# The residual of the output projection: an accumulating DMA in place of a load and a VectorE addition

## The chip, the core and the metric

The kernel runs on one core of a Trainium2 chip. The metric is the device time of one launch, in microseconds (us). TensorE (PE in the profile) multiplies matrices, VectorE (DVE) and ScalarE (ACT) work element by element, GpSimd (POOL) and SyncE (SP) do little arithmetic here or none: SP issues DMAs, the transfers between device memory (DRAM) and the core's on-chip memory. Each engine works through its own list of instructions in order, and waits at an instruction until what it needs is there.

## The reference

A two-layer encoder for 512 tokens of width 2048. In each layer `h` is the RMS-normalised `x`, one projection feeds three groups of attention heads (16 heads in all), the heads' outputs are multiplied by gates, and one output projection is added to `x`. A final RMS norm follows.

```python
for l in range(DEPTH):                       # DEPTH = 2
    h = rms_norm(x, norm_g[l])
    z = h @ w_in[l]
    ...                                      # three kinds of attention: o_na, o_dl, o_m
    y = jnp.concatenate([o_na * jax.nn.silu(na_g), o_dl * jax.nn.silu(dl_g), o_m * jax.nn.silu(m_g)], axis=-1)
    x = x + y @ w_out[l]
return rms_norm(x, final_g)
```

The change concerns the last line of the loop: how `x +` is done.

## The kernel before

**Layout.** Activations lie transposed: 16 tiles (`KO`) of 128 model columns by 512 tokens, f32. Every product is made of three products of split operands: `split` (L179, L180) writes `hi`, the operand rounded by a ScalarE cast, and `lo`, the rest, by a VectorE subtraction; `mm3` (L204 to L206) multiplies hi·hi, hi·lo, lo·hi.

**Weights.** A weight tile is 128 output columns by all 2048 rows, streamed in two halves of 128 x 1024. `next_half` keeps `AHEAD` = 3 halves loaded (SP, L153) and split (ACT L179, DVE L180) ahead of the one in use; the raw halves `wr` and both parts `wh`, `wl` have four buffers each (`W_BUFS`). So the cast of a half can begin when the half four places before it has been used up, and its result is wanted three halves later. In the program a half's load and split come ahead of the products that use the half three places before it.

**The stage of the change.** At the end of a layer a loop over `j` makes the new `x` tile by tile (L511 to L529): 16 tiles in layer 0, 13 in layer 1 (the last three of layer 1 are made in two halves of the tokens by `project`, which the change leaves alone). For tile `j`, SP loads the old `x` (L520; from the input `xT` in layer 0, from the scratch `xs` in device memory in layer 1) into a tile `p`; TensorE computes the projection `acc` in 48 products (`gemm_t`, L521); VectorE adds both into `x` (L523). What follows from `x`:

- `add_square` (L524): ScalarE squares the tile (L242 or L245), VectorE adds the square into `ssq` (L247), the sum that the next RMS norm needs.
- in layer 0, SP stores `x` to `xs` (L526), and `act_tile` (L527) multiplies it by the norm's gain and splits it for the next layer (ACT L185, DVE L186);
- in layer 1, ScalarE multiplies it by the final gain (L529).

**Behind the stage.** Layer 1's first product (`gemm_v`) starts right after layer 0's last tile. It takes the new tiles in order, two for each half of a weight tile, and at its second half `rms_scales` comes in: TensorE sums `ssq` down the partitions (L267), VectorE makes the reciprocal root (L252 to L258, L274), TensorE spreads it (L275), ScalarE copies it to `rstd` (L277).

**What sets the order.** The code is one stream of instructions; a scheduler spreads it over the engines' lists, moving a few instructions by its own estimate of times, and inserts the waits. GpSimd has nothing to do in the loop; its list holds attention masks before it and the two products of the rotary tables (L480, L481) behind it.

Of the kernel before, what the change touches and what calls it, by code (L numbers as in the profile page):

```python
# [14 lines left out]
ALU = mybir.AluOpType  # L15
# [5 lines left out]
T = 512  # L21
D = 2048
# [5 lines left out]
EPS = 1e-6  # L28
NEG = -1e30
ROWS = 8  # L30
W_HALF = 1024  # columns of half a weight tile
W_BUFS = 4  # halves of weight tiles on chip, as loaded and in each of their two parts
AHEAD = 3  # halves that are loaded and split ahead of the one in use
U_BUFS = 62  # [128, 512] tiles for everything that lives longer than a few instructions
LAST = 3  # column tiles of the last projection that are computed for one half of the tokens after the other
WARM = 10  # products of constants ahead of the first loads' arrival
# Microseconds of TensorE's work from a head's operands to its first scores, between its steps, and from
# its last scores to its first transposes.
NA_TIMES = (5.0, 1.2, 3.0)
DIL_TIMES = (8.0, 1.3, 4.0)  # L40
MEM_TIMES = (4.0, 0.7, 3.5)
# Tiles of x that are loaded along with each of the first halves of the weights.
FIRST_LOADS = (1, 3, 2, 2, 2, 2, 2, 2)

# Column tiles of one layer's weights, in the order in which they are streamed: "T" tiles hold 128
# output columns and all of K, "V" tiles 512 output columns and a quarter of K.
SEQ = (
# [14 lines left out]
for _key in SEQ:  # L62
    WPOS[_key] = sum(4 if s in ("v", "mv") else 1 for s, _ in SEQ[:len(WPOS)])
# Mix tiles (heads) in the order in which gates are applied: memory, neighbourhood, dilated.
MIX = [("m", h) for h in range(H_M)] + [("na", h) for h in range(H_NA)] + [("dl", h) for h in range(H_DL)]
# Neighbourhoods of a query block of 16 grid columns: the key tiles that they touch, the first of the 32
# columns that they span, where these columns' biases start in a head's window, and their mask.
NA_KB = [(0, 2), (0, 3), (1, 4), (2, 4)]
# [7 lines left out]
def hybrid_kernel(ctx: ExitStack, tc: tile.TileContext, xT, memT, gains, rpbw, wts, cs_tab, dil_tab, na_tab, outT):  # L76
# [35 lines left out]

# [1 line left out]
    ones = cpool.tile([P, P], F32, tag="ones", name="ones")  # L114
# [15 lines left out]
    ssq = cpool.tile([P, T], F32, tag="ssq", name="ssq")  # L130
    # TensorE's clock is raised by work: raise it while the first loads are under way.
    bank = sc_bank()
# [3 lines left out]

# [1 line left out]
    stream = []  # L138
# [38 lines left out]
    def split(x, hi, lo):  # L177
        """x as hi + lo."""
        nc.scalar.copy(hi, x)  # L179
        nc.vector.tensor_tensor(lo, x, hi.bitcast(F32), ALU.subtract)  # L180
        return hi, lo

    def split_scaled(x, g, hi, lo):
        """x * g (one g per partition) as hi + lo."""
        nc.scalar.activation(hi, x, AF.Copy, scale=g)  # L185
        nc.vector.scalar_tensor_tensor(lo, x, g, hi.bitcast(F32), ALU.mult, ALU.subtract)  # L186
        return hi, lo

    # Attention is issued in steps between the matmuls of later products. A step is due when TensorE has
    # had work for so many microseconds since the head's operands were issued that its inputs are there.  # L190
    clock = [0.0]
# [10 lines left out]
    def mm3(out, a, b, start, stop):  # L202
        """out += a.T @ b for a = a[0] + a[1], b = b[0] + b[1]."""
        nc.tensor.matmul(out, lhsT=a[0], rhs=b[0], start=start, stop=False)  # L204
        nc.tensor.matmul(out, lhsT=a[0], rhs=b[1], start=False, stop=False)  # L205
        nc.tensor.matmul(out, lhsT=a[1], rhs=b[0], start=False, stop=stop)  # L206
        clock[0] += 3 * out.shape[-1] / 2400.0

    def gemm_t(l, key, act, n=T):
        """[128 columns, n tokens] of one T tile."""  # L210
        acc = acc_bank()
        for half in range(2):
            hi, lo = next_half(l, key)
            for k8 in range(8):
                ko = half * 8 + k8
                sl = slice(k8 * P, (k8 + 1) * P)
                mm3(acc[:, :n], (hi[:, sl], lo[:, sl]), act[ko], ko == 0, ko == KO - 1)
                pump()
        return acc

    def gemm_v(l, key, act, ntok, hook=None):
        """[ntok x 128 tokens, 512 columns] of one V chunk."""
        accs = [acc_bank() for _ in range(ntok)]
        for q in range(8):
            hi, lo = next_half(l, key)
            if hook is not None:
                hook(q)
            for t in range(ntok):
                ts = slice(t * P, (t + 1) * P)
                for kk in range(2):  # L230
                    ko = 2 * q + kk
                    sl = slice(kk * 512, (kk + 1) * 512)
                    mm3(accs[t], (act[ko][0][:, ts], act[ko][1][:, ts]), (hi[:, sl], lo[:, sl]),
                        ko == 0, ko == KO - 1)
                    pump()
        return accs

# [1 line left out]
    def add_square(src, first, n=T, acc=None):  # L239
# [9 lines left out]
    def rsqrt(out, src_ps, n):  # L249
        """out = (src / D + EPS) ** -0.5"""  # L250
        a = sb.tile([P, 4], F32, tag="rs", bufs=4, name=nm("rs"))[:, :n]
        nc.vector.tensor_scalar(a, src_ps, 1.0 / D, EPS, ALU.mult, ALU.add)  # L252
        u = sb.tile([P, 4], F32, tag="rs", bufs=4, name=nm("rs"))[:, :n]
        nc.vector.tensor_scalar(out.bitcast(I32), a.bitcast(I32), -0.5, 1597463007.0, ALU.mult, ALU.add)
        for _ in range(3):
            nc.vector.tensor_tensor(u, out, out, ALU.mult)
            nc.vector.scalar_tensor_tensor(u, u, -0.5, a, ALU.mult, ALU.mult)
            nc.vector.scalar_tensor_tensor(out, u, 1.5, out, ALU.add, ALU.mult)  # L258

    def rms_scales(bc, tok, n, *accs):  # L260
        """1 / rms of each token: down the partitions in tok, along every partition's row in bc.
        The sum of accs holds the squares, to be summed down the partitions."""
        nt = n // P
# [15 lines left out]

# [1 line left out]
    def attend(q, score, v, order, first, gap, wait):  # L281
        """Queue a head's steps and return its tile of outputs [hd, queries].
        score(qt): probabilities of a query tile; order: key tile, [(query tile, its column there)]."""
        out, probs, pts, bank = [], {}, {}, []
# [37 lines left out]
    def softmax(s, neg_max, scale, src):  # L322
        """s = exp(scale * src + neg_max) over its row's sum."""
        l = stat()
        nc.scalar.activation(s, src, AF.Exp, bias=neg_max, scale=scale, accum_out=l)  # L325
        r = stat()
        nc.vector.reciprocal(r, l)
        nc.vector.tensor_scalar(s, s, r, None, ALU.mult)
# [53 lines left out]

# [1 line left out]
    def act_tile(l, ko, x):  # L384
# [10 lines left out]
    for l in range(NL):  # L395
# [15 lines left out]
        def beside_first(q):  # L411
            """What runs beside a layer's first product: norms, the memory's split, layer 0's loads and splits."""
            if l == 0:
                tiles = range(len(act), min(2 * q + 4, KO))
                for ko in tiles:
                    act.append(act_tile(0, ko, xraw[ko]))
                for ko in tiles:
                    add_square(xraw[ko], ko == 0)
            if q == (6 if l == 0 else 1):
                rms_scales(rstd, rstd_tok, T, ssq)  # L420
# [71 lines left out]

        # gates
        mix = []
# [13 lines left out]

        # output projection, residual, and what follows from a tile of the new x
        act = []  # L510
        out = []  # L511
        kept = []
        for j in range(KO if l + 1 < NL else KO - LAST):
            if l + 1 == NL and j == KO - LAST - 4:
                for c in range(4):
                    raw = u32()
                    nc.sync.dma_start(out=raw, in_=wts[l, WPOS["o", KO - LAST], :, c * T:(c + 1) * T])
                    kept.append(split(raw, u32r(), u32r()))
            old = f32t("p", 4)
            nc.sync.dma_start(out=old, in_=xT[j] if l == 0 else xs[j])  # L520
            acc = gemm_t(l, ("o", j), mix)  # L521
            x = u32()
            nc.vector.tensor_tensor(x, acc, old, ALU.add)  # L523
            add_square(x, j == 0)  # L524
# [6 lines left out]

# [1 line left out]
    cols = range(KO - LAST, KO)  # L533
# [53 lines left out]
def _tables(np):  # L587
    """Constants of the shapes alone: rotary tables and attention masks."""
    tok = np.arange(T).reshape(ROWS, GRID_W).T.reshape(T)
# [88 lines left out]
```

## Time and profile before

| | |
|---|---|
| time, median of 2 runs | 1868.47 us (1868.43 and 1868.52) |
| span of the profiled execution, first to last instruction | 1868.0 us |
| TensorE busy | 1849.4 us (99%) |
| VectorE, ScalarE, GpSimd busy | 1038.4, 659.4, 51.6 us |
| granted TensorE clock, mean | 0.996 of full speed |
| tiles that the change touches | 16 in layer 0, 13 in layer 1 |

The profile is of one execution. Its own time is not listed apart from its span; the runs' median lies 0.47 us above that span, which is what lies around it. A row of a timeline gives the start in us from the first instruction, the duration in us, the engine, the line of the code, the operation, output<-input with the names of the code, and in brackets the idle time ahead of it with what ended it. A group of rows in the tables is one kind of instruction. Matmuls are pipelined, so one matmul of the stage shows 0.39 us although one starts about every 0.23 us.

### The profile page before, as it was taken

What the parts mean: (1) busy time and instruction counts of PE and PEld (TensorE: products, weight loads), DVE (VectorE), ACT (ScalarE), POOL (GpSimd) and SP (SyncE); (2) the same over time, 40 slices, a digit from 0 to 9 for tenths busy, and PEclk for the clock granted to TensorE, in tenths of its full rate; (3) what the DMA queues carried; (4) which work ended last, traced back from release to release, by engine and by line L of the source; (5) the groups of instructions that cost most, each with busy time, mean ns of one, the idle gap of its engine ahead of it and who ended that gap; (6) DMA issues with size and microseconds to landing.
All of it is one profiled execution on the core that took longest, in us unless ns stands there. A gap on an engine that the chain in (4) does not pass through costs nothing.

```text
span 1868.0 us, 22192 instructions
## 1 busy us (share of the span) xinstructions
PE 1849.4 (99%) x8828; PEld 1548.2 (83%) x8828; DVE 1038.4 (56%) x1577; ACT 659.4 (35%) x1034; POOL 51.6 (3%) x110
## 2 busy tenths in 40 slices
PE   9999999999999999999999999999999999999997
PEld 7888888888888888888888898888888888888887
DVE  7457552564567787543434565435636677883333
ACT  6346442333233323232323453333323333233331
POOL 0113000100000000000000100000000000000000
PEclk9999999999999999999999999999999999999998
DMA  8334423222223333444423353232232233334422
GB/s 288 93 101 150 140 68 101 88 80 80 90 68 103 101 94 98 133 138 146 126 92 93 120 172 101 79 102 70 78 91 79 68 103 101 92 100 124 124 91 91
DMA packets 67175, 198.67 MB, mean 106 GB/s; under 512 B 7040, under 2 KB 16768, under 8 KB 67072
## 3 DMA queue, kind: packets, MB, share of 16 engines
q1 hardware_dynamic: 67072, 197.26, 34.4%
q8 instruction: 69, 1.13, 0.2%
q14 instruction: 34, 0.28, 0.0%
HBM read 188.84 MB, written 8.39 MB: 106 GB/s over the span
## 4 chain that ended last, share of the span: by engine, by line
PE 95%; DVE 2%; DMA 1%; ACT 1%; issue 1%; SPq 0%; DVEq 0%; ACTq 0%
PE acc L204 28%; PE acc L205 28%; PE acc L206 28%; PE sc L294 2%; PE pv L205 1%; PE pv L204 1%; PE pv L206 1%; PE sc L205 1%; PE sc L206 1%; PE sc L204 1%; DVE u L186 1%; DMA wr<-in_wts 1%; DMA u<-in_memT 0%; DVE wl L180 0%; ACT u L185 0%
## 5 line engine op out<-in xcount | busy, mean ns | idle before, releaser
L204 PE MATMUL acc<-u,wh 128*128 128x512 f32 (+1 forms) x2064 | 786.5, 381 | 0.0
L205 PE MATMUL acc<-u,wh 128*128 128x512 f32 (+1 forms) x2064 | 784.3, 380 | 0.0
L206 PE MATMUL acc<-u,wl 128*128 128x512 f32 (+1 forms) x2064 | 783.6, 380 | 0.0
L179 ACT CAST wh<-wr 128x1024 fp32r<-128x1024 f32 (+1 forms) x319 | 334.8, 1049 | 724.5 <-PE acc L205 401.0
L180 DVE TENSOR_TENSOR wl<-wr,wh 128x1024 fp32r<-128x1024 f32 (+1 forms) x319 | 390.1, 1223 | 319.0 <-ACT wh L179 313.6
L206 PEld LDWEIGHTS acc<-u,wl 128*128 128x128 f32 x2064 | 388.2, 188 | 74.4
L205 PEld LDWEIGHTS acc<-u,wh 128*128 128x128 f32 x2064 | 388.5, 188 | 69.1
L204 PEld LDWEIGHTS acc<-u,wh 128*128 128x128 f32 x2064 | 388.5, 188 | 69.0
L204 PE MATMUL acc<-wh,u 128*128 128x512 f32 x448 | 175.3, 392 | 1.3 <-ACT u L185 1.3
L205 PE MATMUL acc<-wl,u 128*128 128x512 f32 x448 | 174.9, 390 | 0.0
L206 PE MATMUL acc<-wh,u 128*128 128x512 f32 x448 | 174.4, 390 | 0.0
L180 DVE TENSOR_TENSOR ptl<-sc,pth 128x512 fp32r<-128x512 f32 (+2 forms) x112 | 67.4, 603 | 89.7 <-ACT pth L179 89.2
L501 DVE RECIPROCAL tmp<-tmp 128x512 f32<-128x512 f32 x32 | 107.2, 3351 | 1.0
L179 ACT CAST pth<-sc 128x512 fp32r<-128x512 f32 (+2 forms) x112 | 57.9, 517 | 122.6 <-PE sc L294 119.9
L204 PEld LDWEIGHTS acc<-wh,u 128*128 128x128 f32 x448 | 84.2, 188 | 17.9 <-ACT u L185 1.5
L206 PEld LDWEIGHTS acc<-wh,u 128*128 128x128 f32 x448 | 84.1, 188 | 18.0
L205 PEld LDWEIGHTS acc<-wl,u 128*128 128x128 f32 x448 | 84.1, 188 | 16.9 <-DVE wl L180 0.4
L325 ACT ACTIVATE p<-p,stat 128x256 f32<-128x256 f32 (+1 forms) x96 | 59.1, 616 | 87.2 <-DVE stat L335 86.4
L523 DVE TENSOR_TENSOR u<-acc,p 128x512 f32<-128x512 f32 x29 | 20.0, 691 | 89.3 <-PE acc L206 89.3
L179 ACT CAST u<-tmp 128x512 fp32r<-128x512 f32 (+1 forms) x64 | 37.7, 591 | 67.2 <-DVE tmp L438 67.2
L294 PEld LDWEIGHTS sc<-ident,p 128*128 128x128 f32 x376 | 48.0, 140 | 15.0
L294 PE MATMUL sc<-ident,p 128*128 128x128 f32 x376 | 59.8, 272 | 0.0
(98 smaller groups left out, 1237.1 us busy)
## 6 DMA issues: line engine op xcount, KB each, us to landing
wr<-in_wts SPq DMA_DIRECT2D x317, 512.0 KB, 3.7
p<-in_xT SPq DMA_DIRECT2D x32, 256.0 KB, 3.5
u<-in_memT SPq DMA_DIRECT2D x16, 256.0 KB, 4.4
xs<-u SPq DMA_DIRECT2D x16, 256.0 KB, 2.0
p<-xs SPq DMA_DIRECT2D x13, 256.0 KB, 2.7
outT<-wr SPq DMA_DIRECT2D x6, 512.0 KB, 3.6
e<-in_rpbw SPq DMA_DIRECT2D x12, 192.0 KB, 2.4
u<-in_wts SPq DMA_DIRECT2D x4, 256.0 KB, 4.2
```

What stands on the lines that cost most here:

```text
L179: nc.scalar.copy(hi, x)
L180: nc.vector.tensor_tensor(lo, x, hi.bitcast(F32), ALU.subtract)
L186: nc.vector.scalar_tensor_tensor(lo, x, g, hi.bitcast(F32), ALU.mult, ALU.subtract)
L204: nc.tensor.matmul(out, lhsT=a[0], rhs=b[0], start=start, stop=False)
L205: nc.tensor.matmul(out, lhsT=a[0], rhs=b[1], start=False, stop=False)
L206: nc.tensor.matmul(out, lhsT=a[1], rhs=b[0], start=False, stop=stop)
L294: nc.tensor.transpose(tr[:, i * P:(i + 1) * P], probs[qt][:, col:col + P], ident)
L325: nc.scalar.activation(s, src, AF.Exp, bias=neg_max, scale=scale, accum_out=l)
L501: nc.vector.reciprocal(e, e)
L523: nc.vector.tensor_tensor(x, acc, old, ALU.add)
```

## The change

The load of the old `x` on SP and the tile `p` for it are gone. ScalarE copies the product from `acc` to `x`, and a DMA issued by GpSimd adds the old `x` from device memory onto `x` where it lies on the chip. The lines behind it are the same and now take `x` when this DMA has ended. In the changed file the lines from here on have numbers one lower (the copy is L521, the DMA L522, the store to `xs` L525). The rest of the diff takes comments out of the file.

```diff
-            old = f32t("p", 4)
-            nc.sync.dma_start(out=old, in_=xT[j] if l == 0 else xs[j])
             acc = gemm_t(l, ("o", j), mix)
             x = u32()
-            nc.vector.tensor_tensor(x, acc, old, ALU.add)
+            nc.scalar.copy(x, acc)
+            nc.gpsimd.dma_start(out=x, in_=xT[j] if l == 0 else xs[j], accum_op=ALU.add)
             add_square(x, j == 0)
             if l + 1 < NL:
                 nc.sync.dma_start(out=xs[j], in_=x)
```

How the lists of the engines move is shown at two places. The first is ScalarE around the last tile of layer 0 (`j` = 15). Before, with `u_7388` the new `x`, `tmp_7390` its square and `u_7394` its part for the next layer; the casts `wh` are weight halves:

```order
L179 CAST wh_7359<-wr_7358 128x1024
L179 CAST wh_7403<-wr_7402 128x1024
L245 ACTIVATE tmp_7390<-u_7388 128x512
L185 ACTIVATE u_7394<-u_7388,g_sb 128x512
L179 CAST wh_7433<-wr_7432 128x1024
L277 COPY rstd<-sc_7456 128x512
```

The same place of the changed kernel, where `u_7371` is the new `x`:

```order
L179 CAST wh_7342<-wr_7341 128x1024
L179 CAST wh_7387<-wr_7386 128x1024
L521 COPY u_7371<-acc_7310 128x512
L245 ACTIVATE tmp_7374<-u_7371 128x512
L185 ACTIVATE u_7378<-u_7371,g_sb 128x512
L179 CAST wh_7417<-wr_7416 128x1024
L277 COPY rstd<-sc_7440 128x512
```

One row is new, the copy; it stands behind the cast that stood ahead of the square, and the square is next to it. Every tile of the loop in layer 0 has this pattern of two casts, copy, square, gain.

The second place is SP's list in layer 0 around three stores of new tiles. Before, `p` is the load of an old tile:

```order
L153 DMA wr_6409<-in_wts 128x1024
L526 DMA xs<-u_6295 128x512
L520 DMA p_6522<-in_xT 128x512
L153 DMA wr_6452<-in_wts 128x1024
L153 DMA wr_6482<-in_wts 128x1024
L526 DMA xs<-u_6366 128x512
L520 DMA p_6595<-in_xT 128x512
```

And of the changed kernel:

```order
L153 DMA wr_6447<-in_wts 128x1024
L525 DMA xs<-u_6293 128x512
L153 DMA wr_6477<-in_wts 128x1024
L153 DMA wr_6519<-in_wts 128x1024
L525 DMA xs<-u_6363 128x512
```

The loads of old tiles are gone from SP's list, and each store stands one weight load later. On GpSimd the 16 accumulating DMAs of layer 0 stand together between the last attention mask of layer 0's list and the rotary products (L480, L481), and the 13 of layer 1 at the list's end. TensorE's list is the same but for the four L275 of layer 1's norm, which stand two products later; VectorE's loses the 29 additions, and a few weight subtractions stand one or two places from where they stood.

## Rows read from the trace of the kernel before

**Rows 1.** The page: span, and busy time, share and instructions of each engine

```profile
span 1868.0 us, 22192 instructions
PE 1849.4 (99%) x8828; PEld 1548.2 (83%) x8828; DVE 1038.4 (56%) x1577; ACT 659.4 (35%) x1034; POOL 51.6 (3%) x110
```

**Rows 2.** The page: the chain that ended last, by engine

```profile
PE 95%; DVE 2%; DMA 1%; ACT 1%; issue 1%; SPq 0%; DVEq 0%; ACTq 0%
```

**Rows 3.** Windows: layer 0's loop, most of layer 1's, the end; columns in the first line

```profile
core 0: us, PE busy (x) PEld busy (x) DVE busy (x) ACT busy (x) POOL busy (x), PEclk, DMA share, GB/s
767.00:930.30 163.30, 163.30 (x722) 135.23 (x721) 65.51 (x74) 48.90 (x61) 0.00 (x0) 1.00 0.45 140
...
1683.00:1804.00 121.00, 121.00 (x535) 100.21 (x534) 43.61 (x48) 39.47 (x48) 0.00 (x0) 1.00 0.43 130
1804.00:1868.00 64.00, 51.29 (x378) 48.78 (x376) 24.18 (x71) 11.23 (x19) 0.00 (x0) 0.89 0.20 66
```

**Rows 4.** Waits of TensorE, first and last of five: for whom, total us, times, longest

```profile
PE sc L275 <- DVE tmp L274: 4.2, 3, 2.6
...
PE sc L267 <- ACT tmp L555: 0.4, 1, 0.4
```

**Rows 5.** Timeline of VectorE from layer 0's tile 14 to the norm

```profile
919.42 0.69 DVE L523 TENSOR_TENSOR u<-acc,p 128x512 f32<-128x512 f32 x1 [3.31 <-PE acc L206]
...
930.30 0.69 DVE L523 TENSOR_TENSOR u<-acc,p 128x512 f32<-128x512 f32 x1 [3.35 <-PE acc L206]
931.16 1.23 DVE L180 TENSOR_TENSOR wl<-wr,wh 128x1024 fp32r<-128x1024 f32 x1 [0.17 <-ACT wh L179]
932.30 0.68 DVE L247 TENSOR_TENSOR ssq<-ssq,tmp 128x512 f32<-128x512 f32 x1
```

**Rows 6.** Timeline of ScalarE over the same stretch

```profile
930.07 1.05 ACT L179 CAST wh<-wr 128x1024 fp32r<-128x1024 f32 x1 [4.38 <-PE acc L205]
931.03 0.62 ACT L245 ACTIVATE tmp<-u 128x512 f32<-128x512 f32 x1
931.56 0.71 ACT L185 ACTIVATE u<-u,g_sb 128x512 fp32r<-128x512 f32 x1
...
941.31 0.59 ACT L277 COPY rstd<-sc 128x512 f32<-128x512 f32 x1 [4.48 <-PE sc L275]
```

**Rows 7.** Timeline of TensorE: layer 1's first product and its norm

```profile
930.10 0.39 PE L204 MATMUL acc<-wh,u 128*128 128x512 f32 x1
...
935.32 0.39 PE L206 MATMUL acc<-wh,u 128*128 128x512 f32 x1
935.54 0.95 PE L267 MATMUL sc<-ones,ssq 128*128 128x1 f32 x8
936.35 0.49 PE L204 MATMUL acc<-wh,u 128*128 128x512 f32 x1
```

**Rows 8.** DMAs by line, first the loads of `p` in layer 0's loop, then the stores

```profile
L520 SPq DMA_DIRECT2D p<-in_xT x12: 328/423/425, 768.5 to 887.9; - x12
...
DMA to landing us min/median/max: 2.6/2.9/4.8
...
L526 SPq DMA_DIRECT2D xs<-u x16: 326/326/331, 767.8 to 931.0; - x16
...
DMA to landing us min/median/max: 2.0/2.0/2.3
```

**Rows 9.** Timeline of GpSimd behind layer 0's loop

```profile
941.98 1.29 POOL L480 TENSOR_TENSOR rope_c<-rope_c,rstd 128x512 f32<-128x512 f32 x1 [570.36 <-ACT rstd L277]
```

**Rows 10.** Timeline of SP at layer 0's last tile

```profile
931.02 0.33 SPq L526 DMA_DIRECT2D xs<-u  x1
932.41 40.84 SPq L153 DMA_DIRECT2D wr<-in_wts  x8
```

**Rows 11.** Line L523 in the whole trace: durations in ns min/median/max

```profile
L523 DVE TENSOR_TENSOR u<-acc,p x29: 683/692/692, 767.1 to 1815.3; 128x512 f32<-128x512 f32 x29
```

## The prediction

> **What bounds the kernel now.** I read the page's totals first. TensorE is busy for 1849.4 us of a span of 1868.0 us [rows 1], so all other engines together hold it up for only 18.6 us. The chain that ended last is 95% TensorE [rows 2], and the list of TensorE's waits holds five short ones, none longer than 2.6 us and none for a weight half or for a tile of the new `x` [rows 4]. Next the windows: in layer 0's loop TensorE is busy for 163.30 of 163.30 us at granted clock 1.00 (2.4 GHz); ScalarE works 48.90 us there, VectorE 65.51 us, GpSimd nothing [rows 3]. Layer 1's loop, of which the second window is most, has no idle TensorE either. So the stage that the change edits is paced by TensorE alone, and an edit off TensorE can win nothing there. It can lose, at a place where TensorE soon needs what comes out of the loop. The timelines show the tightest such place: behind layer 0's last tile. I therefore read the three engines there.
>
> The last two additions start at 919.42 and 930.30 [rows 5]: a tile lasts 10.88 us, a weight half 5.44 us. After tile 15, layer 1's first product starts at once (930.10), and 5.44 us later, at 935.54, TensorE comes to L267, which sums `ssq` [rows 7]. `ssq` is complete at 932.30 + 0.68 = 932.98 [rows 5]. **The slack is 935.54 - 932.98 = 2.56 us.**
>
> **The change, part by part.**
>
> *Removed.* 29 VectorE additions at 0.692 us, 20.1 us [rows 11], and 29 loads on SP with 0.33 to 0.42 us of issue each [rows 8]. VectorE is idle 3.3 us ahead of each addition [rows 5] and SP is not waited for, so this is worth 0.
>
> *Added on ScalarE.* 29 copies from `acc`. The nearest row is L277, also a copy of 128x512 out of TensorE's accumulators: 0.59 us [rows 6], 17.1 us in all. ScalarE does 48.90 / 15 = 3.26 us a tile in the 15 tile periods of layer 0's window [rows 3]; with the copy 3.85 us out of 10.88. That alone costs 0 too.
>
> *Added as a wait.* The square of a tile now waits for copy, GpSimd's issue and the transfer. Call t the time from the copy's end to the square's start. No row of the trace shows t: GpSimd issues no DMA in the loop, and nothing accumulates. The rows near it are the plain load of the same 256 KB, 2.6 to 4.8 us with a median of 2.9, and the store of such a tile, 2.0 us; SP's issue is seen as 0.33 us [rows 8]. An accumulation must read device memory and the tile on the chip, and write the tile. Lower bound: one issue and the quickest of these transfers, 0.33 + 2.0 = 2.3 us. Upper bound: an issue as long as a whole GpSimd operation on such a tile, 1.29 us [rows 9], the slowest load and the slowest store one after the other, 1.29 + 4.8 + 2.3 = 8.4 us. I take the middle reading, both legs at their medians one after the other: **t = 0.33 + 2.9 + 2.0 = 5.2 us**, since the operation does a load's work and moves the tile a second time.
>
> The Trainium skill (DMA: Bandwidth & Descriptors, "Anatomy of one DMA — SWDGE (gpsimd) path") fits a DMA issued from GpSimd as about 2.0 us plus its bytes at 436 GB/s. For 256 KB that makes 2.6 us as an estimate, with which the wait would be just covered and the time 1868.5; no run here shows it, and the fit is of plain copies. The skill's page Collectives: The Full Stack (Part 3) lays the lower rate of a reduction in transfer to its two source reads, which is on the side of the larger t.
>
> *What hides the wait inside the loop.* Behind the waiting square in ScalarE's list stand the gain (L185) and the next two weight casts; VectorE's `ssq` addition and L186 wait too, with weight subtractions behind them. A cast begins when the half four places back is used up (its idle time ends by TensorE, [rows 6]); its result is wanted three halves later, 3 x 5.44 = 16.3 us; cast and subtraction need 1.05 + 1.23 [rows 5, 6]. So 14.0 us of lateness are covered. And a tile's lateness does not pass to the next as long as ScalarE's work and the wait fit into a period: 3.85 + t up to 10.88, so **t up to 7.03 us**. With 5.2, ScalarE is held for 9.05 us of 10.88 and catches up in each tile. Within the loops the price is 0. Where layer 1 prepares its last weight tile, four more casts of 128x512, about 0.62 us each like the square [rows 6], exceed one period by 9.05 + 2.5 - 10.88 = 0.7 us, which the next tile takes up.
>
> *SP.* The store to `xs` waits for the accumulation in place of the addition, and the weight loads behind it wait with it. They now start right behind a split, 932.41 after 931.16 + 1.23 [rows 5, 10], four halves (21.8 us) ahead of their cast; some 5 us of delay are covered. GpSimd has no work in the loop; its next, the rotary products, start at 941.98 after `rstd` [rows 9] and stay where `rstd` is. The accumulation replaces a load of the same bytes, at 0.45 DMA share [rows 3].
>
> *What does not hide it.* At layer 0's end, the cast that begins at 930.07 still stands ahead. The copy takes the square's old place, 931.03, and ends at 931.62; the square starts at 931.62 + t and ends at 932.24 + t. VectorE's addition follows with a handoff of some 0.06 us (I estimate it from 930.99, the end of the addition before, to the square at 931.03 [rows 5, 6]) and takes 0.68, so `ssq` is complete at 932.98 + t. TensorE reaches L267 at 935.54. **Stall = t - 2.56 = 2.7 us**, once. The chain behind L267 (VectorE's root, L275) is shifted whole, and TensorE's products between L267 and L275 cover VectorE's root as before, so nothing more is lost. Layer 1's loop ends differently: its `ssq` is wanted only behind four half tiles of `project`, 4 x 5.44 = 21.8 us after the last tile's end (its addition starts at 1815.3, [rows 11]), so it pays nothing.
>
> The sum: on the profile's span 1868.0 + 2.7 = 1870.7; the runs lie 0.47 us above that span, so 1868.47 + 2.7 = **1871.1 us**.
>
> **The rivals.**
>
> *Hidden altogether.* With t at most 2.56 us, `ssq` is ready when TensorE asks: 1868.5. For it: the lower bound, 2.3, and the 2.0 us of a store. Against it: a load alone takes 2.9 at the median.
>
> *ScalarE becomes the bound (the slower side).* With t over 7.03 us each of 15 periods leaves ScalarE t - 7.03 later, so the last tile's `ssq` comes late by 15 (t - 7.03) + t - 2.56 in all, and TensorE pays that at L267 or, from 14.0 us on, already at a weight half. Layer 1 adds 12 (t - 7.03) + 2.5 - 14.0 where that is positive. At the upper bound, t = 8.4: 20.6 + 5.8 + 4.9 = 31 us, about 1900. It costs 2% (37 us) from t = 8.6 on: 23.6 + 6.0 + 7.3 = 37. For it: the operation is not in the trace, and GpSimd makes the transfer, whose issue I know only from SP; waits of 4.8 us for a plain load occur. Against it: it needs about three median loads' time for 256 KB at a DMA share of 0.45.
>
> *A gain.* The 20.1 us freed on VectorE would count if TensorE waited for VectorE in the loop. It is never idle there [rows 3], and the 12.7 idle us at the end (64.00 - 51.29) lie behind code that the change leaves alone.
>
> **How the numbers follow.** Forecast (t between 2.56 and 7.03; 1868.5 to 1873): 0.72. Hidden: 0.08. ScalarE the bound but under 2% (7.03 to 8.6): 0.08. Over 2%: 0.11. A gain over 2%: 0.01. The prediction is the likeliest, 1871.1. The range takes in the hidden case at 1867.5 and reaches into ScalarE's case up to 1882, which is t = 7.6 (15 x 0.57 + 5.0 = 13.6); beyond it lie some 15 in 100. A change under 2% is about what a measurement of this kernel can't tell from none; so faster 0.01, same 0.88, slower 0.11.
>
> **What would show it.** In the changed profile: TensorE still busy for all of layer 0's loop; one new wait of TensorE, at L267, of t - 2.56; 29 copies of about 0.6 us; ScalarE idle about 5 us ahead of each square, ended by the DMA, and idle again ahead of the first cast behind it. The prediction is wrong if the copies start later and later against the ends of their products, if TensorE waits for weight halves, or if L267 shows no wait.

## The result, and the profile after

The changed kernel takes 1885.73 us (1885.27 and 1886.19), 17.3 us more than before; the ratio is 1.0084, with a 95% interval of 1.0067 to 1.0100. That is under 2%, and outside the range that was forecast (1867.5 to 1882). The span of the profiled execution is 1883.5 us, 15.5 us more than [rows 1].

The page of the changed kernel: span, busy time of the engines, the queue of GpSimd's DMAs (packets, MB, share of 16 engines) and their issues (KB each, median us from issue to landing).

```profile
span 1883.5 us, 22206 instructions
PE 1854.0 (98%) x8828; PEld 1551.7 (82%) x8828; DVE 1018.3 (54%) x1548; ACT 670.0 (36%) x1063; POOL 77.7 (4%) x139
...
q0 software_dynamic: 4176, 7.60, 2.4%
...
u<-in_xT POOLq DMA_DIRECT2D x16, 256.0 KB, 7.3
...
u<-xs POOLq DMA_DIRECT2D x13, 256.0 KB, 7.0
```

VectorE lost 20.1 us of work, as costed. ScalarE's busy time grew by 10.6 us where 17.1 were costed: the 29 copies alone make 16.7, but rows that follow closely overlap, and time in which two overlap counts once. The accumulations need about 7 us to land. TensorE is still busy all through layer 0's loop, as in [rows 3]:

```profile
767.00:930.30 163.30, 163.30 (x722) 135.24 (x721) 52.88 (x56) 51.85 (x72) 13.16 (x15) 1.00 0.50 136
```

The waits of TensorE (total us, times, longest) have two new rows beside those of [rows 4]:

```profile
PE sc L267 <- DVE ssq L247: 6.0, 1, 6.0
PE acc L204 <- ACT u L521: 4.8, 1, 4.8
PE sc L275 <- DVE tmp L274: 4.4, 3, 2.6
```

The first is the wait that was forecast, 6.0 us where 2.7 was written. The second was not: layer 1's first product fills four accumulators at once, and the fourth is the one from which ScalarE still has to copy layer 0's last tile. ScalarE's timeline shows why the copy is late (tiles 1 and 2; L521 is the copy, L245 the square, in brackets the wait ahead of it):

```profile
777.48 1.05 ACT L179 CAST wh<-wr 128x1024 fp32r<-128x1024 f32 x1 [0.87 <-ACT wh L179]
778.43 0.58 ACT L521 COPY u<-acc 128x512 f32<-128x512 f32 x1
786.50 0.63 ACT L245 ACTIVATE tmp<-u 128x512 f32<-128x512 f32 x1 [7.49 <-DMA u<-in_xT]
787.04 0.71 ACT L185 ACTIVATE u<-u,g_sb 128x512 fp32r<-128x512 f32 x1
787.65 1.99 ACT L179 CAST wh<-wr 128x1024 fp32r<-128x1024 f32 x2
789.54 0.57 ACT L521 COPY u<-acc 128x512 f32<-128x512 f32 x1
798.11 0.63 ACT L245 ACTIVATE tmp<-u 128x512 f32<-128x512 f32 x1 [7.99 <-DMA u<-in_xT]
798.65 0.71 ACT L185 ACTIVATE u<-u,g_sb 128x512 fp32r<-128x512 f32 x1
799.26 1.99 ACT L179 CAST wh<-wr 128x1024 fp32r<-128x1024 f32 x2
801.15 0.57 ACT L521 COPY u<-acc 128x512 f32<-128x512 f32 x1
```

From one copy to the next pass 11.11 and 11.61 us, in which ScalarE waits for nothing but the transfer; a tile of TensorE lasts 10.88. Here t, the copy's end to the square's start, is 7.49 and 8.00 us. The list of GpSimd's DMAs gives the sum of the lag (durations of the issue in ns, then first and last start):

```profile
L522 POOL DMA_DIRECT2D u<-in_xT x16: 853/867/1011, 768.5 to 939.1; - x16
```

170.6 us for 15 periods, where 15 x 10.88 = 163.2: the last copy comes 7.4 us late. TensorE's timeline behind it, in the place of [rows 7]:

```profile
933.63 0.39 PE L206 MATMUL acc<-wh,u 128*128 128x512 f32 x1
938.79 0.79 PE L204 MATMUL acc<-wh,u 128*128 128x512 f32 x1 [4.77 <-ACT u L521]
939.38 0.63 PE L205 MATMUL acc<-wl,u 128*128 128x512 f32 x1
...
941.09 0.63 PE L206 MATMUL acc<-wh,u 128*128 128x512 f32 x1
947.69 1.84 PE L267 MATMUL sc<-ones,ssq 128*128 128x1 f32 x8 [5.98 <-DVE ssq L247]
```

The products behind the waits start 0.43 us apart in place of 0.23. The windows show the granted clock (the figure after POOL's):

```profile
930.00:932.00 2.00, 2.00 (x10) 1.68 (x9) 0.00 (x0) 0.00 (x0) 0.00 (x0) 1.00 0.67 165
...
942.00:944.00 2.00, 0.00 (x0) 0.00 (x0) 0.00 (x0) 0.00 (x0) 0.00 (x0) 0.50 0.97 257
...
952.00:954.00 2.00, 2.00 (x6) 1.52 (x6) 1.49 (x8) 0.00 (x0) 0.00 (x0) 0.50 0.67 193
954.00:956.00 2.00, 2.00 (x13) 1.70 (x12) 0.00 (x0) 0.00 (x0) 0.00 (x0) 0.99 0.17 70
```

TensorE stood from about 934 to 938.8, and its clock fell to 0.50 (1.2 GHz) and came back to 0.99 (2.4 GHz) at 954. So the 15.5 us of span are 4.8 + 6.0 of waiting and 4.6 more of busy time (1854.0 against 1849.4), and nearly all of it lies between 934 and 957.

### The profile page after: what moved, and what is told of

Read it like the earlier page. It is cut to its first block, busy times and chain, and to the rows that moved or that the text cites. A ratio compares the mean times of both kernels' runs of the same rounds, so it can differ in the third digit from the quotient of the medians.

```text
span 1883.5 us, 22206 instructions
## 1 busy us (share of the span) xinstructions
PE 1854.0 (98%) x8828; PEld 1551.7 (82%) x8828; DVE 1018.3 (54%) x1548; ACT 670.0 (36%) x1063; POOL 77.7 (4%) x139
## 3 DMA queue, kind: packets, MB, share of 16 engines
q0 software_dynamic: 4176, 7.60, 2.4%
## 4 chain that ended last, share of the span: by engine, by line
PE 86%; issue 6%; DMA 4%; DVE 2%; ACT 2%; POOL 0%; SPq 0%; DVEq 0%; ACTq 0%; POOLq 0%
PE acc L204 25%; PE acc L205 25%; PE acc L206 25%; DMA u<-in_xT 3%; PE sc L294 2%; PE pv L205 1%; PE pv L204 1%; PE pv L206 1%; PE sc L206 1%; PE sc L205 1%; PE sc L204 1%; ACT wh L179 1%; DVE wl L180 1%; ACT u L185 1%; DVE u L186 1%
## 5 line engine op out<-in xcount | busy, mean ns | idle before, releaser
L247 DVE TENSOR_TENSOR ssq<-ssq,tmp 128x512 f32<-128x512 f32 x42 | 28.9, 689 | 186.0 <-ACT tmp L245 186.0
L205 PEld LDWEIGHTS acc<-wl,u 128*128 128x128 f32 x448 | 85.0, 190 | 17.1 <-DVE wl L180 0.5
L245 ACT ACTIVATE tmp<-u 128x512 f32<-128x512 f32 (+1 forms) x42 | 23.1, 550 | 193.6 <-DMA u<-in_xT 116.6
```

What stands on the lines that cost most here:

```text
L245: nc.scalar.activation(sq, src, AF.Square)
L247: eng.tensor_tensor(acc[:, :n], acc[:, :n], sq, ALU.add)
```

## The experiments

Four theories stood at the start. **The wait**: ScalarE, held at each square for a transfer longer than its period allows, falls behind, and TensorE pays for it once, behind layer 0's last tile. Against it: **the copy** (its place on ScalarE costs by itself), **traffic** (the transfers slow the weights, all through both loops), and **the last transfer alone** (no lag, only t ahead of L267). The kernel before, run along, took 1869 to 1872 us from one set of runs to the next, and its spans were 1867.7 to 1870.6. Spans are compared below (1868.0 before, 1883.5 with the change), but one span alone is known to no better than 2 us or so; what rests on less is read from rows.

**The copy alone.** SP's load and VectorE's addition are back, behind ScalarE's copy.

```diff
+            old = f32t("p", 4)
+            nc.sync.dma_start(out=old, in_=xT[j] if l == 0 else xs[j])
             ...
-            nc.gpsimd.dma_start(out=x, in_=xT[j] if l == 0 else xs[j], accum_op=ALU.add)
+            nc.vector.tensor_tensor(x, x, old, ALU.add)
```

> ScalarE copies the product, SP loads the old tile as before, and VectorE adds it in place: the copy without the accumulating DMA. Theory 'ScalarE waits for the transfer in order' (called the wait): nothing but 0.6 us of ScalarE is added per tile and no wait, so 1868.5 within 1 us. Rival 'the copy itself, and its place behind a weight cast, is what costs' (called the copy): about 1885.

Measured: 1869.81 us, span 1868.0, the same as before, and no new wait; the 1.3 us above the expected 1868.5 lie outside the span. The copy is not the cause.

**Each layer alone.** The DMA under `if l == 0` or `if l == 1`, the old lines in the other layer.

> The accumulating DMA in layer 0's 16 tiles only; layer 1 loads and adds as before. The wait: all of the loss inside the span lies behind layer 0's last tile, so the span keeps the +15.5 us, about 1882 to 1884, and the time is about 1884 to 1886. Rival 'it is spread over all 29 tiles': +16/29 of 17.3, about 1878.

> The accumulating DMA in layer 1's 13 tiles only. The wait: ScalarE falls behind there too, but nothing is wanted of it before the lag is made up; span +0 to 1.5 us, and the time about 1869 to 1871.5, the last 1.3 us of it outside the span if the use of GpSimd's DMA queue costs that. Rival 'spread over all 29 tiles': +13/29 of 17.3, about 1876.

Measured: layer 0 alone 1882.79 us, span 1881.0, of the 15.5 us 13.0, a little under what was expected; its waits are 7.7 us at L267 and 3.8 for the accumulator. Part of the missing 2.5 us is a shorter stretch ahead of the first changed line: the first copy starts at 766.0, in the changed kernel at 767.55. Layer 1 alone 1871.69, span 1869.9, with no new wait of TensorE, although ScalarE waits there as in the changed kernel's layer 1 (75.5 us in 12 squares, there 77.0). Some 1.5 us of its 1.9 are a first stretch that is longer before any changed line runs (L267 of layer 0 starts at 41.1 in place of 39.6), which differs among the profiles. The loss is behind layer 0.

**Whether GpSimd's queue costs something by itself.** One load of 32 KB issued by GpSimd in the kernel before.

```diff
-    nc.sync.dma_start(out=g_sb, in_=gains)
+    nc.gpsimd.dma_start(out=g_sb, in_=gains)
```

> The kernel before, with one small load of 32 KB (the gains) issued by GpSimd in place of SP. If the use of GpSimd's DMA queue as such costs the 1.3 us that the changed kernel's runs lie further above their spans (1.8 against 0.45), the time is about 1869.8 and the span 1868.0; if not, 1868.5.

Measured: 1869.84 us, span 1868.1, the very figures that the idea gave. But `copy_only`, which uses no DMA of GpSimd, lay as far above its span (1.8 us), and so did the kernel before, run beside both (1871.91, span 1870.1). So the 1.3 us outside the span belong to the set of runs and not to the queue; the idea fell.

**Followers one tile later.** Square, sum, store, gain and split of tile `j` are issued behind the copy and the DMA of tile `j` + 1.

```diff
-            add_square(x, j == 0)
-            ...
+            if j > 0:
+                follow(l, j - 1, new[j - 1])
+            new.append(x)
+        follow(l, len(new) - 1, new[-1])
```

> The accumulating DMA as in the change, but all that takes the new tile (square, sum, store, gain and split) is issued one tile later, behind the next tile's copy and DMA. The wait: ScalarE no longer stands at an unfinished transfer inside the loop and does not fall behind; what is left is the last tile's transfer ahead of L267, 3 to 6 us, and products at half clock behind that idle time, up to 3 us: 1873 to 1878, no wait of TensorE for the copy. Rival 'the transfers slow the weights' (called traffic): the same transfers at the same places, so still about 1885.

Measured: 1880.31 us, span 1878.5. The wait for the accumulator is gone, as expected, the one at L267 is not smaller:

```profile
PE sc L267 <- DVE ssq L247: 6.1, 1, 6.1
```

The scheduler moved the squares forward again, ahead of the next casts, so that ScalarE still stands at each. Only the gain (0.72 us) came behind the next copy, and so out of the circle of copy, transfer, square, casts and next copy (L531 is the copy here, L532 the DMA):

```profile
779.45 0.58 ACT L531 COPY u<-acc 128x512 f32<-128x512 f32 x1
779.92 0.73 ACT L185 ACTIVATE u<-u,g_sb 128x512 fp32r<-128x512 f32 x1
786.94 0.63 ACT L245 ACTIVATE tmp<-u 128x512 f32<-128x512 f32 x1 [6.30 <-DMA u<-in_xT]
787.48 1.04 ACT L179 CAST wh<-wr 128x1024 fp32r<-128x1024 f32 x1
```

The first and last start of its accumulations in layer 0, as above:

```profile
L532 POOL DMA_DIRECT2D u<-in_xT x16: 856/866/1011, 769.5 to 933.4; - x16
```

That much was enough: 163.9 us for 15 periods, a lag of 0.7 in place of 7.4. With as many and as long transfers as in the change (7.4 us to landing) the accumulator wait went, which speaks against traffic. The 6.1 us left are the last tile's own: its square starts 7.98 us after its copy, and 7.98 + 0.7 - 2.56 = 6.1. The expectation failed in taking t as 5 to 6 there.

**The norm later**, by itself and with the late followers.

```diff
-            if q == (6 if l == 0 else 1):
+            if q == (6 if l == 0 else 4):
```

> The change, with layer 1's norm (L267 and what follows) at the fifth half of its first product in place of the second, 16 us later. The wait: ScalarE is as late as in the change; TensorE still waits 4.8 us for the last tile's accumulator, and no longer for the sum; with a few products at half clock about 1876 to 1879. Rival 'only the last transfer ahead of L267 counts': the loss is gone, 1869 to 1870.

> Both: the followers one tile later and layer 1's norm 16 us later. The wait: neither the accumulator nor the sum is late, TensorE has no new wait, and what is left is what lies outside the span: 1868.5 to 1870. Traffic: about 1885 less the wait at L267 (6.0), 1879.

Measured: norm later alone 1878.26 us, span 1876.5. The wait at L267 is gone and the one for the accumulator is there:

```profile
939.90 0.79 PE L204 MATMUL acc<-wh,u 128*128 128x512 f32 x1 [6.14 <-ACT u L521]
940.49 0.63 PE L205 MATMUL acc<-wl,u 128*128 128x512 f32 x1
```

6.1 us of it and 1.9 us of products at half clock (nine, from 939.90 to 943.85) make 8.0 of the 8.5. So "only the last transfer counts" fell: the lag alone costs. Both together: 1871.74 us, span 1870.0, with no new wait, at 7.4 us from issue to landing. That is more than the 1868.5 to 1870 that were expected, in a single run; it was timed again:

> late_norm again, timed in rounds beside the kernel before. The theory that all of the loss is TensorE's wait behind layer 0's last tile (and the half clock behind it): 1.000 to 1.001 of before. If accumulating DMAs cost something more that is spread over the run: 1.002 or more. No gain is expected of it, since TensorE paces the run.

Measured: 1870.74 us against 1870.61 before, ratio 1.0001 with 0.9991 to 1.0011. Every transfer of the change is in it, with TensorE never waiting for one. What the change cost is thus the waits behind layer 0's last tile with the slow products that follow them, and nothing spread over the run that would exceed the interval's 2 us.

**What makes the transfer long.** In four runs parts of it are taken away. In `no_loads` and `no_loads_plain` layer 0's projection splits its weights from one tile that stays on the chip; in `plain_pool` and `no_loads_plain` the DMA of GpSimd overwrites instead of adding, and in `plain_act` it does so from ScalarE's queue.

```diff
+        if layer == 0 and at >= WPOS["o", 0]:
+            split(fixed[:, None, :].to_broadcast([P, 2, T]), ...)
+            return hi, lo
```

```diff
-            nc.gpsimd.dma_start(out=x, in_=xT[j] if l == 0 else xs[j], accum_op=ALU.add)
+            nc.gpsimd.dma_start(out=x, in_=xT[j] if l == 0 else xs[j])      # plain_pool, no_loads_plain
+            nc.scalar.dma_start(out=x, in_=xT[j] if l == 0 else xs[j])      # plain_act
```

> The change, but the weight halves of layer 0's output projection are not loaded: each is split from one tile that stays on the chip, so the projection's values are left out, and the work of the engines is the same. If the 7 to 8 us of a transfer in the loop are its own, ScalarE falls behind as in the change, about 1885. If they come from the 1 MB of weights that are loaded at the same time, a transfer takes 4 to 5 us from the copy's end to the square, as at the end of layer 1 (4.4 to 4.6), ScalarE keeps pace, and only the last tile's 2 to 3 us at L267 are lost: 1871 to 1875.

> As the change, but GpSimd's DMA writes the old tile over the copy in place of adding it (the projection is left out of the result): the same queue, issue and waits, without the second reading and the addition. If the accumulation makes the transfer long, t (copy's end to square) falls from 7.7 to about 5, ScalarE keeps pace, and the span is about 1871 to 1874. If the queue of GpSimd beside the weight loads makes it long, t stays at 7 to 8 and the span at about 1882.

> As plain_pool, but ScalarE issues the overwriting DMA (the projection is left out of the result): the hardware's queue, no step over GpSimd. If GpSimd's queue is what is slow, t is 3.5 to 4.5 us, no lag, span 1869 to 1872. If the weight loads at the same time are what is slow, whichever queue is used, t is 5.5 to 7, and the span lies between 1871 and 1880.

> GpSimd's DMA overwrites (the projection is left out of the result) and layer 0's projection loads no weights, as in no_loads. Against the 4.4 us of an accumulation without weight loads this gives what the accumulation itself costs: if its second leg is worth a store, 2.0 us, t is 2.4; if the addition runs along with the transfer, t is 3.5 to 4.4.

The lines of the four, one view after the other (in the two runs without loads the line numbers are 5 higher): ScalarE's timeline in `no_loads`, then the list of its accumulations in layer 0 (durations in ns, first and last start); the queue of `plain_pool` on its page (packets, MB, share), then its list; the list of `plain_act`; queue and issues of `no_loads_plain` on its page.

```profile
781.62 0.58 ACT L526 COPY u<-acc 128x512 f32<-128x512 f32 x1
786.68 0.63 ACT L250 ACTIVATE tmp<-u 128x512 f32<-128x512 f32 x1 [4.48 <-DMA u<-in_xT]
787.22 0.71 ACT L190 ACTIVATE u<-u,g_sb 128x512 fp32r<-128x512 f32 x1
787.84 1.03 ACT L184 CAST wh<-fixed 128x1024 fp32r<-128x1024 f32 x1
```

```profile
L527 POOL DMA_DIRECT2D u<-in_xT x16: 853/868/1013, 771.7 to 934.9; - x16
```

```profile
q0 software_dynamic: 2320, 7.60, 1.7%
```

```profile
L522 POOL DMA_DIRECT2D u<-in_xT x16: 536/536/707, 768.8 to 932.1; - x16
```

```profile
L522 ACTq DMA_DIRECT2D u<-in_xT x16: 334/334/383, 768.1 to 931.3; - x16
```

```profile
q0 software_dynamic: 2320, 7.60, 1.5%
...
u<-in_xT POOLq DMA_DIRECT2D x16, 256.0 KB, 2.9
```

In all of them 15 periods last 163.2 or 163.3 us: with a short t there is no lag. From ScalarE's rows, t as a mean over the first eight tiles of layer 0:

| t in layer 0's loop | beside weight loads | without them |
|---|---|---|
| overwrite, ScalarE's queue | 2.81 us | not run |
| overwrite, GpSimd's queue | 3.84 us | 3.37 us |
| add, GpSimd's queue | 7.59 us | 4.42 us |

GpSimd's queue costs 1.0 us; the addition 1.0 us without weight loads; and beside them an addition loses 3.2 us where an overwrite loses 0.5. GpSimd's issue is not what grows: it takes 0.87 us in the changed kernel and in `no_loads` alike.

The traffic in the middle column is not the same, though. Each weight tile comes in two halves. In the changed kernel both go off within 2 us of an accumulation (shown further down); in `plain_pool` one goes off 0.5 us behind the overwrite and the other 3.3 us or more ahead of it. Only the first tile is like for like, with one half 0.5 us behind the DMA in both. The squares of that tile in the changed kernel, in `plain_pool`, in `no_loads` and in `no_loads_plain`:

```profile
774.42 0.63 ACT L242 ACTIVATE ssq<-u 128x512 f32<-128x512 f32 x1 [6.29 <-DMA u<-in_xT]
```

```profile
772.88 0.63 ACT L242 ACTIVATE ssq<-u 128x512 f32<-128x512 f32 x1 [4.38 <-DMA u<-in_xT]
```

```profile
775.81 0.63 ACT L247 ACTIVATE ssq<-u 128x512 f32<-128x512 f32 x1 [4.49 <-DMA u<-in_xT]
```

```profile
773.87 0.63 ACT L247 ACTIVATE ssq<-u 128x512 f32<-128x512 f32 x1 [3.37 <-DMA u<-in_xT]
```

So beside one half the addition loses 1.8 us and the overwrite 1.0; in the changed kernel's layer 0 the longer times, 7.1 to 8.3, occur where two halves go off about the accumulation. How an overwrite fares beside two was not run.

Measured: `plain_pool` span 1871.4, `plain_act` 1868.3, `no_loads_plain` 1872.0, `no_loads` 1880.6. The last two start 2 to 3 us late, since their extra tile is loaded first (TensorE waits 2.6 and 2.9 us for the first operands, 1.3 before); and behind the loop layer 1's weights are loaded, so in `no_loads` the last tile's t is 7.76 again. Its expectation of 1871 to 1875 missed that; there was no lag, as it said. Both overwrites were quicker than either case of their expectations (t of about 5 or 7 to 8, and 3.5 to 4.5 or 5.5 to 7). The four check the other half of the sum too: TensorE's wait at L267 was forecast as t - 2.56. By the last tile's t it should be 0.23, 1.08, 1.02 and 5.20 us, and it is 0.2, 1.0, 1.0 and 5.2.

**Whether the lag feeds itself.** In the changed kernel both halves of a weight tile are sent off about the next accumulation, one 0.4 to 1.4 us ahead of its start and one 0.5 to 0.7 us behind it, since both splits stand behind the same square (SP, then GpSimd, changed kernel; SP's rows stand for two issues, the second at 779.82 and 791.11):

```profile
777.89 2.25 SPq L153 DMA_DIRECT2D wr<-in_wts  x2
...
789.97 1.46 SPq L153 DMA_DIRECT2D wr<-in_wts  x2
...
779.32 0.87 POOL L522 DMA_DIRECT2D u<-in_xT  x1 [9.84 <-ACT u L521]
790.41 0.86 POOL L522 DMA_DIRECT2D u<-in_xT  x1 [10.22 <-ACT u L521]
```

Before, the two lie 5.4 us apart. The second half now lands 6.3 to 7.4 us after its issue, where a half took 3.5 to 4.9 before; nobody waits for it. The run `side` is the kernel before with a second copy of each product onto which an accumulation goes that nobody waits for:

```diff
             nc.vector.tensor_tensor(x, acc, old, ALU.add)
+            side = f32t("p", 4)
+            nc.scalar.copy(side, acc)
+            nc.gpsimd.dma_start(out=side, in_=xT[j] if l == 0 else xs[j], accum_op=ALU.add)
```

> The kernel before, and beside it, with nobody waiting for it, a second copy of each product onto which GpSimd's DMA adds the old tile. ScalarE does not fall behind, so the weight halves are loaded one by one, 5.4 us apart, as before. If an accumulation beside weight loads takes 7 us or more whatever their spacing, its time from issue to landing stays at 7 (7.3 in the changed kernel). If the lag feeds itself, by sending both halves of a weight tile off just ahead of the next accumulation, it falls to 5 to 6 here, near the 6.3 from copy to square of the changed kernel's first tile. TensorE waits for nothing new and the span is 1868 to 1869 either way.

Measured: 1871.19 us, span 1869.4, and no new wait. From issue to landing:

```profile
p<-in_xT POOLq DMA_DIRECT2D x16, 256.0 KB, 6.7
...
p<-xs POOLq DMA_DIRECT2D x13, 256.0 KB, 5.8
```

Against 7.3 and 7.0 in the change. In layer 0 a load and a store of 256 KB each run at the same time too, in layer 1 the load only. So the answer is between the two expectations: beside weights that come one by one an accumulation takes about 6, the pairing adds about 1. Neither layer of `side` matches the changed kernel's traffic, so this 1 us is no more than an estimate. The first tiles say the same: ahead of any lag t is 6.3 us in layer 0 (6.28 to 6.35 in six runs), under the 7.3 from which ScalarE falls behind (worked out in the next section). So the pairing, which the first wait brings about, is likely what carries t over that threshold; no run keeps ScalarE's waits and takes the pairing away.

## Why the prediction was wrong

- **What bounds the kernel** was right: no engine but TensorE counts in the loops; ScalarE's copies (0.58 us measured, 0.59 forecast) cost nothing, as `copy_only` shows, and VectorE's 20.1 us freed win nothing, as `late_norm` shows.
- **The place** was right: the loss lies at layer 0's end, at L267, and layer 1's loop pays nothing. **The slack** of 2.56 us was right too, to 0.1 us in four runs.
- **The step that failed is t.** It was put at 0.33 + 2.9 + 2.0 = 5.2 us from one SP issue and the medians of a load and a store. Measured in the loop: 7.6 in the mean of the first eight tiles, 7.7 of all 16. Without weight loads it would have been enough (4.4); what was missing is the weight loads themselves, beside which an accumulation took 6.3 us with one half and 7.1 to 8.3 with two. The row of the plain load gave no sign of it: each of those loads ran beside a weight half too, and ten of the twelve landed within 2.9 us. With the term went the step built on it, that ScalarE catches up in each tile and the price within the loops is 0. The upper bound of 8.4 held, but it was given too little weight.
- **So the rival decided.** With t over 7.03, ScalarE is the bound. Its formula gives 15 x 0.57 + 5.0 = 13.6 us for t = 7.6 and 14.9 for 7.68, the mean of all 16 tiles. TensorE began L267 12.5 us later than 5.44 us after layer 1's start (947.69 against 929.78 + 5.44): the lag of 7.4, and 7.5 - 2.56 = 4.9 for the last tile's t. The formula comes out 1.1 to 2.4 us high, and its threshold of 7.03 is a little low: ScalarE's circle is 3.6 us beside t (11.61 - 8.00), so the lag starts at 7.3. The chance of 0.08 for this case was too small, and the range ended inside it.
- **Not in any case: the accumulator.** Said was that lateness shows at L267 or at a weight half. The first stop was the fourth accumulator, from some 2.5 us of lag on: layer 1's first product takes all four, the fourth 4.1 us after its start (18 products of 0.227 us), where the copy without lag ends after 1.5. It adds nothing as long as L267 comes behind it, because the sum's time decides; in `norm_later` it is the whole loss.
- **Not in any case: the clock.** Idle time of TensorE was priced at its own length. The 10.8 us of waiting were followed by products at clock 0.50, another 4.6 us of busy time. Of the 15.5 us, 12.5 are the delay of L267, slow products ahead of it included, and about 2.8 the slow products behind it (955.54 - 947.69 to L275, where it was 940.15 - 935.54, less two products that stand ahead of it now); the rival's sum has no term for these. Of the 17.3 us of time, 1.8 lie outside the profile's span: 1.3 belong to the set of runs (`pool_gains`), 0.5 to the difference between the changed kernel's two runs.
- **The skill's fit** (the Trainium skill, DMA: Bandwidth & Descriptors, "Anatomy of one DMA — SWDGE (gpsimd) path"), 2.6 us for 256 KB, is near the overwriting transfer without other traffic: 2.9 us from issue to landing. For an accumulation it is no guide: 4.1 without and 7.3 with weight loads. The section does not say of which transfers its fit was taken. The same page of the Trainium skill says under "Issuing engines are not separate DMA queues" that DMAs from all engines share the same 16 DMA engines and interleave. That transfers took longer together than apart here (1.8 us more for an accumulation beside one half; 6.3 to 7.4 us for the second half of a pair in place of 3.5 to 4.9) agrees with that. Why an accumulation suffers more than an overwrite no run here separates. The queue's rows show 144 packets for each accumulation (4176 / 29) and 80 for each overwrite (2320 / 29); whether the count is the reason is open.

## What to carry to other kernels

A wait that an engine meets in order is free only up to its period less its own work; past that, each turn leaves it later, and the bill comes where another engine next needs it, here one layer's end. So price a new transfer by the busiest neighbours it will have, ask what its own lateness does to their timing, weigh the case in which it exceeds that room, and look for every resource that the next stage takes from the late engine, accumulators too. An accumulating DMA can be neutral when its readers stand far enough behind it (`late_norm`, 1.0001), but where TensorE paces the run there is nothing that it can win.

## What the runs showed of the hardware

- An accumulating DMA of 256 KB from GpSimd took 4.4 us from the copy's end to its reader without weight loads, 6.3 beside one weight half of 512 KB and 7.1 to 8.3 where two were sent off within 2 us of it. An overwriting one took 3.4 without weight loads, 4.4 beside one half in the same place and 3.8 in the mean beside halves 4 to 5 us apart; the same from ScalarE's queue 2.8, beside halves 5.4 us apart.
- The second half of such a pair, sent off 0.5 to 0.7 us behind the accumulation, landed after 6.3 to 7.4 us; before, a half took 3.5 to 4.9.
- GpSimd was occupied 0.87 us for issuing an accumulation and 0.54 us for an overwrite.
- Behind 4.8 us without products (the changed kernel) and 6.1 us (`norm_later`) TensorE's granted clock was 0.50, and products of 128x512 started 0.43 us apart in place of 0.23 until it was back at 0.99: about 15 us later with a second wait in between, about 4 us after TensorE resumed without one (`norm_later`, full pace again from 943.9).
